# A head loop with the last head's DMA transposes turned back to TensorE, its loads on one queue, and a few steps moved by half a product

## The chip, the core and the metric

The kernel runs on one core of a Trainium2 chip. The metric is the device time of one execution in microseconds (us); lower is better. The core has TensorE (PE, its weight loads shown as PEld), VectorE (DVE), ScalarE (ACT), GpSimd (POOL) and SyncE (SP), each with an instruction queue of its own that it works off in order. DMAs are issued by SyncE and, some, by GpSimd.

## What is computed

Two layers of a decoder trunk over 1024 tokens of width 1024: dilated attention and an MLP, then gated linear attention and an MLP. The change lies in the first layer's attention. Cut to that:

```python
DILATED_GROUPS = ((128, 1), (512, 4), (2048, 16))   # three branches g = 0, 1, 2; 8 heads of 128
def dilated_attention(h, w_in, w_out):
    qkv = (h @ w_in).reshape(B, S, N_GROUPS, 3, ATTN_HEADS, HEAD_DIM)
    for g, (window, dil) in enumerate(DILATED_GROUPS):
        q = apply_rope(qkv[:, :, g, 0], cos, sin) * (HEAD_DIM ** -0.5)
        k = apply_rope(qkv[:, :, g, 1], cos, sin)
        o_g, lse_g = dilated_group_attention(q, k, v, dil, window // dil)
    alpha = jax.nn.softmax(jnp.stack(lses, axis=0), axis=0)
    o = jnp.sum(alpha[..., None] * jnp.stack(outs, axis=0), axis=0)
    return o.reshape(B, S, ATTN_WIDTH).astype(h.dtype) @ w_out
```

## The kernel before, in words

Values are made earlier. The head loop (`Heads.run_head`, L1184) then runs through 24 groups p = 3h + g, one for each head h and branch g. A group makes q and k of its head and branch as one 2 x 2 block product by a Strassen-Winograd scheme with seven products, S0 to S6 in the order of SLOTS: S0 into bank X, S1 into Y, S3 into V, S2 onto X, S6 onto V, S4 onto X, S5 into Z. (The names in the trace: pX<-s2 is S2, pX<-s3 is S4, pV<-s4 is S6.) Each fp32 product is three matmuls of rounded parts (high and low). Every product is issued in two halves, and after each half `advance` (L947) moves a clock by one and issues what an agenda holds for that step, in order of rank, the lower first. A group has 14 steps; c is its first, so c + 14 is step 0 of the next group. The agenda fixes only the order in each engine's queue: an engine that is not waiting runs ahead of the clock.

In a group with start c (`Heads.plan`, L1158): `keep` copies bank X by ScalarE to e1, e2, e3 (steps 3, 9, 13) and V to e5 (step 7); TensorE may add to X again only when the copy before it has been made. `column` (L1124) adds two banks into a quarter of q or k and issues two DMAs (`cw<-c`, L1130 and L1131) that swap its upper and lower 64 partitions; four steps later VectorE's `turn` (L1138, L1139, L1146) applies the rotary tables and writes qT or kT. One column, of q, is due in step c + 15, that is step 1 of the next group. `load` (L1115) fetches the weights of the next group by four DMAs of 256 KB in step 1, `stage` cuts them from step 8 on.

Attention of a group follows one group later (`follow`, L1196; `Attention.plan`, L1084), in four pairs of query blocks j = 0 to 3: scores (L989) from step 8, softmax on VectorE and ScalarE (L1003, L1005), then P must be transposed. For the second branch TensorE does it (`turn`, L1016, with ScalarE's copy L1018). For the first and third branch it is done by DMA: ScalarE splits P into 16-bit halves (L1035), GpSimd's queue writes them to DRAM (`pscr`, L1037), and SyncE issues a DMA transpose back (`flip`, L1048). Then TensorE multiplies P by V (`values`, L1069), ScalarE copies the result (`orow`, L1073) and SyncE stores it to `og`. Entries of POINTS are the steps of scores, turn or halves, values, and flips.

From the second group of the next head on, `plan_merges` (L1302) merges a head's three branches: it loads the rows of `og` (L1209, 780 KB, half 0 in step 0 of the third group), VectorE computes the weights (L1216, L1217, L1222 to L1225), ScalarE scales twelve slices (L1229, steps 6 to 9), VectorE adds them, and SyncE stores to `oscr`.

In the last group, p = 23, the output projection's weights (`W.dma`, 4 x 512 KB) and the first merged rows (`ol`, 1 MB, L1294) are loaded through GpSimd's queue in steps 1 to 3; ScalarE and VectorE prepare the weights in steps 5 to 8 (L152, L153), and TensorE transposes `ol` in step 8 (L260). `tail` (L1781) spreads the attention of group 23 over the output projection's blocks; two steps of the agenda run after each block.

Of the kernel before, what the change touches and what calls it, by code (L numbers as in the profile page):

```python
# [20 lines left out]
P = 128  # L21
# [4 lines left out]
HEADS = 8  # L26
HD = 128
AW = HEADS * HD
NG = 3
# [13 lines left out]
def hybrid_trunk(ctx, tc, x, norm_mix, norm_mlp, norm_fin, a_in, a_out, g_in, g_up, g_b, g_nw,  # L43
                 g_out, m_up, m_down, tab, msk, gmask, ident_d, out):
    nc = tc.nc
    pe, act, dve, pool, sp = nc.tensor, nc.scalar, nc.vector, nc.gpsimd, nc.sync
# [7 lines left out]
    def h8(shape, dt, name):  # L54
        return wk.tile(shape, dt, name=name, tag="h8", bufs=12)

    def k4(shape, dt, name):
        return wk.tile(shape, dt, name=name, tag="k4", bufs=25)

    def t2(shape, dt, name):  # L60
        return wk.tile(shape, dt, name=name, tag="t2", bufs=8)
# [50 lines left out]
    class Weights:  # L112
# [14 lines left out]
            self.slots.append(src)  # L127
            self.by.append(by)

        def dma(self, by=None):  # L130
            n = self.ndma
            if n < len(self.slots):
                self.ndma += 1
                src = self.slots[n]
                self.raws[n] = k4([P] + list(src.shape[1:]), F32, "raw")
                (by or sp).dma_start(self.raws[n], src)

        def prep(self, eng=dve):
            n = self.nprep
# [41 lines left out]
    W = Weights()  # L181
# [8 lines left out]
    def add_rows(w, k0, by=None):  # L190
        for k in range(2):
            W.add(w[P * (k0 + k):P * (k0 + k + 1), :], by and by(k0 + k))
# [93 lines left out]
    class Split:  # L286
# [4 lines left out]
        @staticmethod  # L291
        def at(tiles, k):
            n = 4 // len(tiles)
            return tiles[k // n][:, k % n, :]
# [442 lines left out]
    oscr = drp.tile([S, D], F32, name="oscr")  # L737
# [209 lines left out]
    def advance():  # L947
        clock[0] += 1
        for _, fn in sorted(agenda.pop(clock[0], []), key=lambda e: e[0]):
            fn()  # L950
# [9 lines left out]
    def load_values(g, h):  # L960

        v = k4([P, NB, HD], F32, "v")
        c = slice(HD * h, HD * h + HD)
        if g == 0:
            sp.dma_start(v, vscr.rearrange("(b p) g c -> p b g c", p=P)[:, :, 0, c])
        elif g == 1:
            for b in range(2):
                sp.dma_start(v.rearrange("p (r b) c -> p r b c", b=2)[:, :, b, :],
                             vscr[512 * b:512 * b + 512].rearrange("(p r) g c -> p r g c", r=4)[:, :, 1, c])
        else:  # L970
            sp.dma_start(v, vscr.rearrange("(p r) g c -> p r g c", r=8)[:, :, 2, c])
        return v
# [6 lines left out]
    class Attention:  # L979
# [102 lines left out]
                    sp.dma_start(to.rearrange("(p r) c -> p r c", r=8)[:, 2 * j - 2:2 * j + 2, :], row)  # L1082

        def plan(self, c, points, turn, values, flip=None):  # L1084
            self.by_dma = flip is not None and self.g in (0, 2)
            if flip is not None and not self.by_dma:
                turn, values = (12, 12, 16, 16), (16, 16, 18, 18)

            def get():
                self.v = load_values(self.g, self.h)  # L1090
            at(c + points[0] - 2, get)
            for j in range(4):
                t = c + points[j]
                at(t, lambda j=j: self.scores(j), 2)
                at(t + 1 + (j % 2 and points[j] == points[j - 1]), lambda j=j: self.soft(j), 2)
                if self.by_dma:
                    at(c + turn[j], lambda j=j: self.halves(j), 3)
                    at(c + flip[j], lambda j=j: self.flip(j), 3)
                else:
                    at(c + turn[j], lambda j=j: self.turn(j), 3)  # L1100
                at(c + values[j], lambda j=j: self.values(j), 4)

    class Heads(Up):
# [54 lines left out]
        def plan(self, p):  # L1158
            c = 14 * p
            st = self.st.setdefault(p, {})  # L1160
            self.behind = True

            def keep(b, name):
                def fn():
                    e = t2([P, 512], F32, name)
                    act.activation(e, st[b], AF.Copy)  # L1166
                    st[name] = e
                return fn
            at(c + 3, keep("X", "e1"), 0)
            at(c + 5, lambda: self.column(p, 0, 0, st["Y"], st["e1"]), 1)  # L1170
            at(c + 7, keep("V", "e5"), 0)
            at(c + 9, keep("X", "e2"), 0)
            at(c + 11, lambda: self.column(p, 1, 0, st["V"], st["e2"]), 1)
            at(c + 13, keep("X", "e3"), 0)
            at(c + 13, lambda: self.column(p, 1, 1, st["X"], st["e5"]), 1)
            at(c + 15, lambda: self.column(p, 0, 1, st["Z"], st["e3"]), 1)
            if p == 0:
                for s, t in ((4, 1), (6, 3), (5, 5)):
                    at(c + t, lambda s=s: self.stage(p, s), 7)
            at(c + 1, lambda: self.load(p + 1))  # L1180
            for s, t in ((0, 8), (1, 9), (2, 10), (3, 11), (4, 14), (6, 15), (5, 17)):
                at(c + t, lambda s=s: self.stage(p + 1, s), 7)

        def run_head(self, p):  # L1184
            self.plan(p)
            if p:
                self.follow(p - 1, 14 * p, self.POINTS if p < self.count - 1 else self.SINGLE)
            for s in self.SLOTS:
# [1 line left out]
                    self.product(p, s, range(2 * half, 2 * half + 2))  # L1190
                    advance()

        POINTS = (8, 8, 12, 12), (11, 12, 15, 16), (21, 21, 25, 25), (14, 15, 18, 19)
        SINGLE = (8, 10, 12, 14), (12, 14, 16, 18), (14, 16, 18, 20)

        def follow(self, p, c, points):  # L1196
# [91 lines left out]
                reached.add((0, half))  # L1288
            at(clock[0] + 7, last)

    def ahead_h8(pairs, by=sp):

        t = h8([P, 4, 512], F32, "ol")
        by.dma_start(t, oscr[512 * pairs:512 * pairs + 512, 0:512].rearrange("(b p) c -> p b c", p=P))  # L1294
        return [t[:, 0:2, :], t[:, 2:4, :]]

    def ahead_k4(p):
# [4 lines left out]
    def plan_merges(h, c):  # L1302

        rows, part = {}, {}

        def load(half):
            rows[half] = merge_load(h, half)

        def weigh(half):
            part[half] = merge_weights(rows[half])  # L1310

        def join(half):
            del part[half]
            merged(h, half, merge_join(rows.pop(half), dve))
        for half in range(2):
            t = c + 14 + 11 * half
            at(t, lambda half=half: load(half))
            if half and h == HEADS - 2:
                t += 8
            at(t + 4, lambda half=half: weigh(half), 9)  # L1320
            at(t + 5, lambda half=half: merge_shares(rows[half], *part[half]), 9)
            for n in range(4):
                at(t + 6 + n, lambda half=half, n=n: merge_scale(rows[half], part[half][1], n), 9)
            at(t + 10, lambda half=half: join(half), 9)
# [383 lines left out]
    for i, n in enumerate(plan[:-5]):  # L1708
# [5 lines left out]
        if n == vals.STEPS - 2:  # L1714
            heads = Heads(vals.h)
# [38 lines left out]
    ol = []  # L1754
    turned = Turned(ol, x[0])
    for p in range(heads.count):
        h, g = divmod(p, NG)
        if g == 1 and h:
            plan_merges(h - 1, 14 * p)
        if p == heads.count - 1:  # L1760
            for k in range(0, KT, 2):
                add_rows(a_out, k)
            c = 14 * p
            at(c + 1, lambda: (W.dma(pool), W.dma(pool)), 0)
            at(c + 2, lambda: (W.dma(pool), W.dma(pool)), 0)
            at(c + 3, lambda: ol.extend(ahead_h8(0, pool)), 0)
            for t in (5, 6, 7, 8):
                at(c + t, lambda: W.prep(dve), 7)
            at(c + 8, lambda: turned.turn(0), 7)
            at(c + 9, lambda: (turned.load_x(0), turned.load_x(1)))  # L1770
            at(c + 11, lambda: turned.turn(1), 7)
            at(c + 17, lambda: ol.extend(ahead_h8(1)), 9)
        heads.run_head(p)
# [7 lines left out]
    def tail():  # L1781

        c = clock[0]
        heads.follow(heads.count - 1, c, ((6, 7, 8, 9), (9, 10, 11, 12), (11, 12, 13, 14)))
        load, start, finish = merges(HEADS - 1, merged)
        rows = {}
        advance()

        def early(half):
            t = rows[half] = h8([P, 4, 512], F32, "ol2")  # L1790
            sp.dma_start(t[:, :, 0:384], oscr[512 * half:512 * half + 512, 512:896].rearrange("(b p) c -> p b c", p=P))
        at(c + 7, lambda: early(0))
        at(c + 16, lambda: early(1))
        for i, (half, h) in enumerate(((0, 4), (0, 5), (0, 6), (1, 4), (1, 5), (1, 6))):
            at(c + (13 + 3 * i if half == 0 else 21 + i), lambda half=half, h=h: t_head(h, half, rows[half][:, :, HD * (h - 4):HD * (h - 4) + HD]))
        at(c + 15, lambda: (load(0), load(1)), 9)
        at(c + 18, lambda: start(0))
        at(c + 19, lambda: finish(0))
        at(c + 20, lambda: start(1))
        at(c + 21, lambda: finish(1))  # L1800
        steps.extend([advance] * 42)

    tail()


# [587 lines left out]
    ol, turn1 = [], []  # L2393
# [81 lines left out]
```

## Time and profile before

| | us |
|---|---|
| median of 3 runs (lowest, highest) | 2601.3 (2597.0, 2602.2) |
| the profiled execution, by its own time | 2598.5 |
| its span | 2596.7 |
| TensorE busy | 2574.3 (99%) |
| VectorE busy | 1864.0 (72%) |
| ScalarE busy | 1298.7 (50%) |
| mean granted TensorE clock | 0.998 |

How to read the lines that follow. A line of the timeline has the start and the length in us, the engine, the source line, the operation and out<-in by the program's names; in brackets stands the idle time of the engine just before it and what ended it. An engine's name with a q is its sequencer, so SPq is the issue of a DMA by SyncE. A line of the waits has who waited for whom, us in total, times, and the longest. A line of the windows has the stretch, its length, and the busy time (and number) of PE, PEld, DVE, ACT and POOL, then the granted clock of TensorE, the busy share of the DMA engines and GB/s. A line of the DMA view has queue, number, KB each, and the median us from issue to landing.

### The profile page before, as it was taken

The page shows a single profiled execution, that of the slowest core. Times are in us where ns is not written, and L with a number is a line of the kernel's source. Part 1 is how long each engine was busy: PE and PEld are TensorE (multiplying, and loading weights), DVE is VectorE, ACT ScalarE, POOL GpSimd, SP SyncE. Part 2 cuts the span into 40 slices and gives each one's busy share as a digit, 9 for nine tenths or more (in the row PEclk, how much of TensorE's full clock was granted, in tenths as well). Part 3 has the DMA queues.
Part 4 walks back from the last instruction along what each step waited for, and adds up shares of the span by engine and source line. Part 5 has one row for each costly group of instructions (what it writes and reads, how often), then busy time and mean ns, then how long its engine had stood idle before and what let it go on. Part 6 is the DMA issues. An engine that isn't in the chain of part 4 may idle for free.

```text
span 2596.7 us, 33212 instructions
## 1 busy us (share of the span) xinstructions
PE 2574.3 (99%) x11985; PEld 2142.2 (82%) x11985; DVE 1864.0 (72%) x3018; ACT 1298.7 (50%) x2360; POOL 51.8 (2%) x81
## 2 busy tenths in 40 slices
PE   9999999999998999999999999999999999999998
PEld 7888888888887888888888888888888888888887
DVE  7745888888887768666657587887657866656567
ACT  6423455656655446555534345654326554553334
POOL 0000000000001000000000000000000000000000
PEclk9999999999999999999999999999999999999999
DMA  5543677777778633554775452463513544396543
GB/s 183 170 141 115 153 179 200 176 201 196 196 205 221 208 122 127 170 168 139 278 260 182 140 195 96 133 200 98 195 65 118 170 157 155 130 356 203 183 149 131
DMA packets 377911, 445.70 MB, mean 172 GB/s; under 512 B 68145, under 2 KB 240561, under 8 KB 377746
## 3 DMA queue, kind: packets, MB, share of 16 engines
q1 hardware_dynamic: 372850, 428.63, 53.5%
q0 software_dynamic: 4752, 14.68, 1.7%
q8 instruction: 94, 1.54, 0.2%
q14 instruction: 71, 0.58, 0.1%
q10 hardware_dynamic: 144, 0.26, 0.0%
HBM read 279.19 MB, written 127.60 MB: 157 GB/s over the span
## 4 chain that ended last, share of the span: by engine, by line
PE 65%; DVE 3%; ACT 1%; DMA 1%; issue 1%; SPq 0%; DVEq 0%; ACTq 0%
PE pB L1938 13%; PE pX L599 10%; PE pA L1938 10%; PE pV L599 7%; PE pY L599 3%; PE pZ L599 3%; PE pd L216 3%; PE pd L214 3%; PE pd L215 3%; PE pB L830 3%; PE pA L830 2%; PE pT L335 1%; DMA cw<-c 1%; PE pO L2236 1%; PE pU L2218 0%
## 5 line engine op out<-in xcount | busy, mean ns | idle before, releaser
L1938 PE MATMUL pB<-dh 128*128 128x512 f32 x512 | 199.4, 389 | 0.0
L1938 PE MATMUL pB<-dh,dl 128*128 128x512 f32 x512 | 199.2, 389 | 0.0
L1938 PE MATMUL pB<-dl,dh 128*128 128x512 f32 x512 | 199.2, 389 | 0.0
L223 DVE TENSOR_TENSOR dl<-sin,dh 128x1024 fp32r<-128x1024 f32 x112 | 136.8, 1221 | 42.4 <-ACT dh L220 41.8
L220 ACT ACTIVATE dh<-sin 128x1024 fp32r<-128x1024 f32 x112 | 117.8, 1052 | 88.4 <-PE pB L1938 33.4
L220 ACT ACTIVATE dh<-kept 128x1024 fp32r<-128x1024 f32 x64 | 67.9, 1061 | 183.3 <-DVE kept L1903 138.1
L599 PE MATMUL pV<-s4h,wd 128*128 128x512 f32 x448 | 150.3, 397 | 0.0
L1938 PE MATMUL pA<-dl,dh 128*128 128x512 f32 x384 | 149.4, 389 | 0.0
L1938 PE MATMUL pA<-dh,dl 128*128 128x512 f32 x384 | 149.4, 389 | 0.0
L1938 PE MATMUL pA<-dh 128*128 128x512 f32 x384 | 149.4, 389 | 0.0
L1005 ACT ACTIVATE pt<-pt,orow 128x128 f32<-128x128 f32 (+1 forms) x192 | 84.7, 443 | 75.7 <-DVE orow L1003 74.4
L1938 PEld LDWEIGHTS pB<-dh 128*128 128x128 f32 x512 | 96.2, 188 | 19.9
L1938 PEld LDWEIGHTS pB<-dl,dh 128*128 128x128 f32 x512 | 96.2, 188 | 19.9
L1938 PEld LDWEIGHTS pB<-dh,dl 128*128 128x128 f32 x512 | 96.1, 188 | 19.8
L537 DVE TENSOR_TENSOR wal<-raw,wah 128x512 fp32r<-128x512 f32 x112 | 76.2, 687 | 40.8 <-ACT wah L536 40.8
L537 DVE TENSOR_TENSOR wbl<-t,wbh 128x1024 fp32r<-128x1024 f32 x56 | 68.6, 1225 | 43.9 <-ACT wbh L536 43.8
L599 PEld LDWEIGHTS pV<-s4h,wd 128*128 128x128 f32 x448 | 84.2, 188 | 19.3 <-ACT e L1166 1.7
L608 ACT ACTIVATE c<-c 128x512 f32<-128x512 f32 x64 | 40.4, 631 | 118.6 <-DVE c L636 77.5
L223 DVE TENSOR_TENSOR dl<-kept,dh 128x1024 fp32r<-128x1024 f32 x64 | 78.4, 1225 | 24.7 <-ACT dh L220 18.7
L599 PE MATMUL pX<-s3h,wgh 128*128 128x512 f32 x224 | 89.3, 399 | 2.4 <-ACT e L1166 2.4
L599 PE MATMUL pZ<-a22h,wgh 128*128 128x512 f32 x224 | 90.1, 402 | 0.0
L599 PE MATMUL pX<-s2h,wbh 128*128 128x512 f32 x224 | 89.0, 397 | 0.0
(400 smaller groups left out, 7378.7 us busy)
## 6 DMA issues: line engine op xcount, KB each, us to landing
sin<-acts SPq DMA_DIRECT2D x112, 512.0 KB, 3.9
raw<-in_mlp_w_up_dram SPq DMA_DIRECT2D x64, 512.0 KB, 6.0
acts<-s SPq DMA_DIRECT2D x64, 512.0 KB, 3.5
raw<-in_mlp_w_down_dram SPq DMA_DIRECT2D x64, 512.0 KB, 4.8
raw<-in_attn_w_in_dram SPq DMA_DIRECT2D x98, 256.0 KB, 4.7
cw<-c SPq DMA_DIRECT2D x192, 128.0 KB, 2.8
acts<-c SPq DMA_DIRECT2D x64, 256.0 KB, 2.2
kept<-in_mlp_w_down_dram SPq DMA_DIRECT2D x32, 512.0 KB, 5.8
```

Of the source, the lines that this page charges most:

```text
L214: pe.matmul(ps, sh, mh, start=start, stop=False)
L215: pe.matmul(ps, sh, ml, start=False, stop=False)
L216: pe.matmul(ps, sl, mh, start=False, stop=stop)
L220: act.activation(hi, src, AF.Copy)
L223: dve.tensor_tensor(lo, src, hi.bitcast(F32), op=OP.subtract)
L335: pe.transpose(ps[:, k, 128 * i:128 * i + 128], xn[i][:, c:c + 128], ident)
L537: self.remain(lambda: dve.tensor_tensor(lo, src, hi.bitcast(F32), op=OP.subtract))
L599: pe.matmul(st[b], u[:, k, :], v, start=first and k + n == 0, stop=k == 3 and n == 2, skip_group_check=True)
L608: act.activation(r, r, AF.Relu)
L830: pe.matmul(self.acc[s][t], a[:, c], b[:, k, :], start=fresh and m + k + v == 0, stop=m == 1 and k == 1 and v == 2, skip_group_check=True)
L1005: act.activation(pt[:, i, :128 * n], pt[:, i, :128 * n], AF.Exp, scale=-1.0, bias=m, accum_out=self.row[:, r, HD:HD + 1])
L1938: pe.matmul(self.acc[s][t], a[:, k, c], b[:, k, :], start=fresh and m + k + v == 0, stop=m == 7 and k == 1 and v == 2, skip_group_check=True)
```

## The change

- The first branch of head 7 is no longer transposed by DMA but by TensorE (`by_dma` also asks for h < 7); its steps become those of the second branch.
- The flips of the other branches: j = 1 moves from step 15 to 14, j = 3 from 19 to 18, so that each pair of flips stands in one step.
- The load of the next group's weights moves from step 1 to step 3.
- The copy e2 of bank X moves from step 9 to step 8 in groups with p mod 3 = 1, but for p = 22.
- The loads of the output weights and of `ol` in group 23 are issued by SyncE instead of GpSimd, in the same steps.
- In the tail, scores, turns and values of group 23 come one step later.

```diff
         def plan(self, c, points, turn, values, flip=None):
-            self.by_dma = flip is not None and self.g in (0, 2)
+            self.by_dma = flip is not None and self.g in (0, 2) and self.h < HEADS - 1
             if flip is not None and not self.by_dma:
                 turn, values = (12, 12, 16, 16), (16, 16, 18, 18)
...
-            at(c + 9, keep("X", "e2"), 0)
+            at(c + (8 if p % NG == 1 and p < self.count - 2 else 9), keep("X", "e2"), 0)
...
-            at(c + 1, lambda: self.load(p + 1))
+            at(c + 3, lambda: self.load(p + 1))
...
-        POINTS = (8, 8, 12, 12), (11, 12, 15, 16), (21, 21, 25, 25), (14, 15, 18, 19)
+        POINTS = (8, 8, 12, 12), (11, 12, 15, 16), (21, 21, 25, 25), (14, 14, 18, 18)
...
-            at(c + 1, lambda: (W.dma(pool), W.dma(pool)), 0)
-            at(c + 2, lambda: (W.dma(pool), W.dma(pool)), 0)
-            at(c + 3, lambda: ol.extend(ahead_h8(0, pool)), 0)
+            at(c + 1, lambda: (W.dma(), W.dma()), 0)
+            at(c + 2, lambda: (W.dma(), W.dma()), 0)
+            at(c + 3, lambda: ol.extend(ahead_h8(0)), 0)
...
-        heads.follow(heads.count - 1, c, ((6, 7, 8, 9), (9, 10, 11, 12), (11, 12, 13, 14)))
+        heads.follow(heads.count - 1, c, ((7, 8, 9, 10), (10, 11, 12, 13), (12, 13, 14, 15)))
```

`W.dma` and `ahead_h8` lose the argument that named the queue; both then issue on SyncE.

More of the change, by code (lines that the diff above doesn't have):

```diff
@@ L128, in add, with dma @@
             self.by.append(by)
-        def dma(self, by=None):
+        def dma(self):
             n = self.ndma
@@ L135, in dma @@
                 self.raws[n] = k4([P] + list(src.shape[1:]), F32, "raw")
-                (by or sp).dma_start(self.raws[n], src)
+                sp.dma_start(self.raws[n], src)
         def prep(self, eng=dve):
@@ L1289, in merged, with ahead_h8 @@
             at(clock[0] + 7, last)
-    def ahead_h8(pairs, by=sp):
+    def ahead_h8(pairs):
         t = h8([P, 4, 512], F32, "ol")
-        by.dma_start(t, oscr[512 * pairs:512 * pairs + 512, 0:512].rearrange("(b p) c -> p b c", p=P))
+        sp.dma_start(t, oscr[512 * pairs:512 * pairs + 512, 0:512].rearrange("(b p) c -> p b c", p=P))
         return [t[:, 0:2, :], t[:, 2:4, :]]
```

## The prediction

> **What bounds the kernel now.** I read the page's busy times first, then TensorE's waits, then windows and timelines around each wait.
>
> ```profile
> span 2596.7 us, 33212 instructions
> PE 2574.3 (99%) x11985; PEld 2142.2 (82%) x11985; DVE 1864.0 (72%) x3018; ACT 1298.7 (50%) x2360; POOL 51.8 (2%) x81
> ```
>
> TensorE is busy 99% of the span, so an edit gains only where it ends one of TensorE's waits, and loses where it starts one or gives TensorE more work. The waits of the head loop are three lines:
>
> ```profile
> PE pO L1069 <- DMA pt<-pscr: 7.0, 5, 5.4
> PE pX L599 <- ACT e L1166: 2.4, 7, 1.1
> PE pS L989 <- DVE qT L1146: 2.2, 3, 1.7
> ```
>
> One wait of 5.4 us is far longer than the rest: TensorE, about to multiply P by V, waits for a DMA transpose (a flip). The timeline puts it into the last group, p = 23, where the flips of head 7's first branch come due. (Groups are called first, second and third by p mod 3.)
>
> ```profile
> 814.84 1.15 POOL L136 DMA_DIRECT2D raw<-in_attn_w_out_dram  x2
> 819.71 1.22 POOL L136 DMA_DIRECT2D raw<-in_attn_w_out_dram  x2
> 821.12 10.34 SPq L1048 DMA_TRANSPOSE pt<-pscr  x2
> 832.63 2.07 PE L1069 MATMUL pO<-v,pt 128*128 128x128 f32 x8 [5.41 <-DMA pt<-pscr]
> 843.25 0.50 PE L599 MATMUL pX<-s3h,wgh 128*128 128x512 f32 x1 [1.08 <-ACT e L1166]
> ...
> 832.00:834.00 2.00, 1.37 (x6) 1.37 (x7) 1.97 (x3) 1.25 (x2) 0.00 (x0) 0.50 1.18 377
> 834.00:836.00 2.00, 2.00 (x8) 1.71 (x7) 1.90 (x6) 0.00 (x0) 0.00 (x0) 0.50 1.02 352
> 836.00:838.00 2.00, 2.00 (x10) 1.61 (x10) 1.35 (x2) 1.84 (x5) 0.00 (x0) 0.73 1.21 163
> ```
>
> Two flips hold SyncE's queue for 10.34 us while 2 MB of output weights land: the DMA share behind the clock column is above 1. TensorE stands 5.41 us, and then runs at a granted clock of 0.50 and 0.73.
>
> The five waits on flips are 7.0 us in all, so the other four hold 1.6 us; they lie in third groups of heads 1 to 6. What sets those groups is another thing. Here are two of them, p = 11 and, below the dots, p = 8:
>
> ```profile
> 514.16 2.51 SPq L1048 DMA_TRANSPOSE pt<-pscr  x2
> 516.77 0.53 SPq L1209 DMA_DIRECT2D rows<-og  x1
> 517.93 0.58 SPq L1131 DMA_DIRECT2D cw<-c  x1
> 518.60 1.95 SPq L1048 DMA_TRANSPOSE pt<-pscr  x1
> 524.02 0.69 DVE L1138 TENSOR_TENSOR cw<-cw,tab 128x512 f32<-128x512 f32 x1 [0.45 <-DMA cw<-c]
> 526.98 0.17 DVE L1225 TENSOR_TENSOR me<-me,mz 128x12 f32<-128x12 f32 x1
> 527.18 0.99 ACT L1229 ACTIVATE rows<-rows,me 128x128 f32<-128x128 f32 x3 [3.97 <-DVE me L1225]
> 530.84 0.69 DVE L1138 TENSOR_TENSOR cw<-cw,tab 128x512 f32<-128x512 f32 x1 [1.86 <-DMA cw<-c]
> 531.31 0.58 ACT L1166 ACTIVATE e<-pX 128x512 f32<-128x512 f32 x1
> 531.94 0.50 PE L599 MATMUL pX<-s3h,wgh 128*128 128x512 f32 x1 [0.20 <-ACT e L1166]
> ...
> 448.01 0.69 DVE L1138 TENSOR_TENSOR cw<-cw,tab 128x512 f32<-128x512 f32 x1 [1.13 <-DMA cw<-c]
> 449.03 1.16 PE L1069 MATMUL pO<-v,pt 128*128 128x128 f32 x8 [0.55 <-DMA pt<-pscr]
> 455.77 0.69 DVE L1138 TENSOR_TENSOR cw<-cw,tab 128x512 f32<-128x512 f32 x1 [2.86 <-DMA cw<-c]
> 455.94 0.50 PE L599 MATMUL pX<-s3h,wgh 128*128 128x512 f32 x1 [0.22 <-ACT e L1166]
> ```
>
> VectorE waits for the swapped rotary rows `cw`, finishes qT, then the merge weights `me`; ScalarE scales the merge rows, and behind them in its queue stands e2, the copy of bank X that TensorE needs. From VectorE's start on cw to TensorE's start on pX it is 531.94 - 524.02 = 7.92 us in the one group and 455.94 - 448.01 = 7.93 in the other, though only the second had a flip wait (0.55). So the landing of cw sets the group; the flip wait lies inside that chain and is worth nothing by itself.
>
> **The change part by part.**
>
> *Head 7 without flips.* Gone are the stand of 5.41 us and the slow clock after it: 1.37 x 0.5 + 2.00 x 0.5 + 2.00 x 0.27 = 2.2 us. Head 7's first branch now needs 3 + 4 + 4 + 4 = 15 transposes on TensorE, 7 in p = 22 and 8 in p = 23. Their price is that of the second branch's transposes:
>
> ```profile
> 770.36 0.82 PE L1016 MATMUL pP<-ident,pt 128*128 128x128 f32 x6
> 771.02 1.50 PE L1069 MATMUL pO<-v,pt 128*128 128x128 f32 x12
> ```
>
> (771.02 - 770.36) / 6 = 0.11 us each, 1.7 us in all, without a new break, since they stand beside scores or values that are there anyway. ScalarE loses the five `halves` and gets four copies. The e2 wait of 1.08 us should fall towards the 0.2 of other third groups: the `orow` copy leaves ScalarE's queue there, but four weight preparations stay. I take 0.9. Sum: -5.4 - 2.2 + 1.7 - 0.9 = **-6.8 us**, with ends at -8.5 (the transposes wholly in slack) and -4 (third rival below).
>
> The rule on the clock in the Trainium skill, TensorE: Matmul & The Clock Gate, Part 1, is that about 3.4 us of idling halve the rate; this trace agrees with its 5.41 us and 0.50, and by the rule none of the waits under 2 us that this change shifts would cost clock.
>
> *Output weights and `ol` from GpSimd's queue to SyncE's.* Four loads and one of 1 MB now stand in SyncE's order, ahead of cw (steps 1 and 5), og and v of p = 23. The trace has the same loads from both queues:
>
> ```profile
> raw<-in_attn_w_out_dram POOLq DMA_DIRECT2D x4, 512.0 KB, 8.9
> raw<-in_attn_w_out_dram SPq DMA_DIRECT2D x4, 512.0 KB, 10.3
> ...
> ol<-oscr POOLq DMA_DIRECT2D x1, 1024.0 KB, 7.9
> ol<-oscr SPq DMA_DIRECT2D x1, 1024.0 KB, 8.2
> ```
>
> 8.9 against 10.3 and 7.9 against 8.2 us to land: about equal. With the five flips of p = 23 gone the queue has room, so I take 0; the upper end is priced as a rival.
>
> *Flips (14, 15, 18, 19) to (14, 14, 18, 18).* In the second and third groups the flip of j = 1 moves ahead of cw of step 1, in third groups ahead of the 780 KB of `rows` too, and the flip of j = 3 ahead of cw of step 5. Queued behind them is everything VectorE's chain waits for. Two flips took 2.51 us of SyncE's queue, so one holds cw back by up to 1.26; the other end is 0, if its transfer hides in DMA time that is idle before rows start (first rival). I take 1.0, nearer the flip's own row. In the six third groups with merges (heads 1 to 6) the chain passes it on whole: **+6.0 us**, ends 0 and +8. The four flip waits go, but what is late next is cw, so they bring nothing. A gain is excluded there unless the chain is wrong (a rival). In second groups TensorE has no wait and no merge stands in ScalarE's queue. Of p = 13, a window row gives its length and the busy time of PE, PEld, DVE, ACT and POOL:
>
> ```profile
> 565.70:589.90 24.20, 24.20 (x118) 20.45 (x117) 20.07 (x42) 14.01 (x34) 3.28 (x5) 1.00 0.76 187
> ```
>
> Busy 24.20 of 24.20 us: 0 from the flips there.
>
> A rule of the Trainium skill speaks against this edit: DMA: Bandwidth & Descriptors, Queues, rings and completion order, says that each engine takes the descriptors of one queue row in ring order. By it the whole transfer of the flip precedes rows and cw and the term would be its upper end; no run here yet shows it.
>
> *Loads of the next weights from step 1 to step 3.* Four DMAs pass the cw of step 1 and, in second and third groups, nothing else that is not moved too; in first groups they pass one og store of two DMAs. They are read at step 8. 0 to +1 us in all, I take 0.
>
> *e2 half a product sooner in second groups.* The row above shows no wait of TensorE in such a group to take away, and the groups that wait (p = 8, 11) are third groups, which the edit leaves alone. ScalarE's weight cut of step 8 comes later by one copy, 0.6 us, and its reader is a group away: 0.
>
> *Tail one step later.* Scores j = 0 waited for qT:
>
> ```profile
> 863.61 0.68 PE L989 MATMUL pS<-kT,qT 128*128 128x128 f32 x4 [1.74 <-DVE qT L1146]
> 864.13 0.83 PE L1069 MATMUL pO<-v,pt 128*128 128x128 f32 x6
> 864.80 0.61 PE L989 MATMUL pS<-kT,qT 128*128 128x128 f32 x4
> ```
>
> Steps 6 and 7 run in the same tick, after the same block, so the scores stay there; only the pO that stood behind them comes first and fills 864.80 - 864.13 = **0.7 us** of the wait (ends 0 and -1.7).
>
> Sum: -6.8 + 6.0 - 0.7 = **-1.5 us**. The profiled execution took 2598.5 us (its span and 1.8 around it), so 2597.0; it lies 2.8 below the median of the runs, 2601.3, on which scale I forecast **2599.8**. Below, 0.2% (5.2 us) is about what a measurement can tell from no change.
>
> **The rivals.**
>
> *Faster: the flips cost nothing.* If the flip of j = 1 runs in DMA time that is idle before rows start, and cw lands as before, only -6.8 - 0.7 = -7.5 is left, and the flip waits may add up to 1.6: 2592 to 2594. For it: SyncE issues rows at 516.77 with only the flips before it. Against: VectorE waits for cw in both groups shown, so no slack absorbs a later issue. Chance 0.22.
>
> *Slower: the second pair of flips carries into the next group.* The cw of step 5 was late too (waits of 1.86 and 2.86 us in the two groups). If the flip of j = 3 ahead of it delays VectorE's scores and merge sums beyond what TensorE itself has lost, the next first group starts late by up to 2.86 - 1.86 = 1.0 us. Six times 1.3 and six times 1.0, less 7.5: +6.3 us, 2607.6. It decides from 2.1 us a head on. Against: TensorE is late by about the same. Chance 0.10.
>
> *The change does not free p = 23.* `ol` behind 2 MB of weights and rows on one queue: it took 8.2 us to land, and TensorE transposes it at step 8, some 14 us into the group. If SyncE gets to it 3 us later than there is room for, TensorE waits for ol in place of the flip, the first term shrinks to -4, and the sum is +1.3: 2602.6. Chance 0.15; it stays within 0.2%.
>
> **How the numbers follow.** The forecast has 0.53. Within 0.2% lie the forecast and the third rival: 0.68; faster 0.22, slower 0.10. The likeliest case's own range, with the flips between +2.3 (where the sum leaves 0.2%) and +8, is -5.2 to +0.5, 2596.1 to 2601.8. The range to hold 8 in 10 takes in the third rival and most of the first: 2593.5 to 2604.5.
>
> **What would show it.** Right: no pO wait on flips in p = 23, clock 1.00 there, 15 more pP transposes; in third groups rows and cw issued about 1.3 us later against the flips, VectorE's wait for cw near 2 us, and the group longer by as much though its pO waits are gone; second groups still 24.2 us. Wrong: third groups as long as before (faster rival), first groups longer by 1 us (slower rival), a pT wait on ol (third rival), or a new wait in second groups.

## The result and the profile after

The changed kernel takes **2629.6 us** (four runs, 2627.8 to 2632.0) against 2600.7 of the kernel before beside it (2597.0 to 2602.2): ratio 1.0114, 95% interval 1.0096 to 1.0131. It is 29 us slower; the forecast was 1.5 us faster, and its range ended at 2604.5. The page of the changed kernel begins so:

```profile
span 2626.3 us, 33210 instructions
...
PE 2583.6 (98%) x12000; PEld 2150.3 (82%) x12000; DVE 1863.9 (71%) x3018; ACT 1296.5 (49%) x2359; POOL 45.5 (2%) x71
```

The work is the same but for 15 matmuls more; the span has grown by 29.6 us. TensorE's waits (who for whom, us in total, times, longest):

```profile
PE pS L989 <- DVE qT L1146: 29.7, 8, 5.9
PE pT L260 <- DMA ol<-oscr: 1.6, 1, 1.6
PE pV L599 <- ACT e L1166: 0.9, 1, 0.9
```

The waits on flips are gone, and the e2 waits in third groups nearly so. In their place the scores wait for qT, 29.7 us where it was 2.2. To see where, I added the lengths of the groups, each from its first matmul to the next group's:

| us | first groups (p = 3 to 21) | second (4 to 22) | third (5 to 20) | p = 23 and all after |
|---|---|---|---|---|
| before | 172.1 | 169.1 | 161.7 | 1779.9 |
| changed | 170.3 | 169.9 | **198.0** | 1774.8 |
| difference | -1.8 | +0.8 | **+36.3** | -5.1 |

Together +30.2; what lies ahead of the groups makes it 29.6. The last group gained 5.1 us; the forecast had 7.5 for it. The six third groups, forecast at +6, lost 36. Here is p = 11 of the changed kernel, which starts at 523.8 (before, the same group started at 514.9): SyncE's queue, then VectorE, then TensorE.

```profile
526.57 3.86 SPq L1048 DMA_TRANSPOSE pt<-pscr  x3
530.52 0.53 SPq L1209 DMA_DIRECT2D rows<-og  x1
531.16 0.61 SPq L1130 DMA_DIRECT2D cw<-c  x1
531.82 0.58 SPq L1131 DMA_DIRECT2D cw<-c  x1
...
538.48 0.17 DVE L1216 TENSOR_REDUCE mz<-rows 128x4 f32<-128x12 f32 x1 [3.33 <-DMA rows<-og]
539.59 0.69 DVE L1138 TENSOR_TENSOR cw<-cw,tab 128x512 f32<-128x512 f32 x1
542.53 0.17 DVE L1225 TENSOR_TENSOR me<-me,mz 128x12 f32<-128x12 f32 x1
...
542.05 2.50 PE L989 MATMUL pS<-kT,qT 128*128 128x256 f32 x6 [5.41 <-DVE qT L1146]
```

Set against the group's start, the flips begin at 2.8 us (before: -0.7), rows are issued at 6.7 (before: 1.9), and VectorE, which now waits for rows and not for cw, ends me at 18.9 (before: 12.3). So the group inherits 3.5 us of lateness, loses 1.3 more to the third flip ahead of rows, and 2.6 more until rows land. The DMA view gives that last part: rows of p = 11, us from issue to landing, before and below it changed.

```profile
rows<-og SPq DMA_DIRECT2D x1, 780.0 KB, 5.3
```
```profile
rows<-og SPq DMA_DIRECT2D x1, 780.0 KB, 7.9
```

3.5 + 1.3 + 2.6 = 7.4 us; the group is 33.3 - 26.5 = 6.8 us longer. TensorE's clock falls too (windows of the changed kernel; the value behind POOL is the granted clock):

```profile
538.00:540.00 2.00, 0.00 (x0) 0.00 (x0) 1.36 (x4) 0.21 (x1) 0.00 (x0) 0.73 1.19 267
540.00:542.00 2.00, 0.00 (x0) 0.00 (x0) 1.97 (x4) 0.00 (x0) 0.00 (x0) 0.50 1.40 267
542.00:544.00 2.00, 1.95 (x6) 1.60 (x6) 1.24 (x8) 1.27 (x4) 0.00 (x0) 0.50 1.11 233
```

Little of that slow stretch shows in the time of this group: me came 6.6 us later and the group is 6.8 longer, so 0.2 is left for the clock. Over the six third groups it is 2.8 of the 36.3 us (worked out below).

Two edits could bring such lateness: the load in step 3 and the flips in pairs. The theory that I formed first was the load (the lateness is there before the group starts); its rivals were the flips, and both together.

### The profile page after: what moved, and what is told of

The parts are those of the page before. It is cut to its first block, busy times and chain, and to the rows that moved or that the text cites. A ratio compares the mean times of both kernels' runs of the same rounds, so it can differ in the third digit from the quotient of the medians.

```text
span 2626.3 us, 33210 instructions
## 1 busy us (share of the span) xinstructions
PE 2583.6 (98%) x12000; PEld 2150.3 (82%) x12000; DVE 1863.9 (71%) x3018; ACT 1296.5 (49%) x2359; POOL 45.5 (2%) x71
## 4 chain that ended last, share of the span: by engine, by line
PE 84%; DVE 6%; DMA 5%; ACT 2%; issue 1%; SPq 1%; DVEq 0%; ACTq 0%
PE pX L599 14%; PE pB L1938 13%; PE pA L1938 10%; PE pV L599 9%; PE pB L830 7%; PE pA L830 5%; PE pZ L599 5%; PE pY L599 5%; PE pd L216 3%; PE pd L214 3%; PE pd L215 3%; DMA rows<-og 2%; DMA cw<-c 1%; PE pS L989 1%; PE pO L1069 1%
## 5 line engine op out<-in xcount | busy, mean ns | idle before, releaser
L989 PE MATMUL pS<-kT,qT 128*128 128x128 f32 (+1 forms) x384 | 76.9, 342 | 29.7 <-DVE qT L1146 29.7
L1138 DVE TENSOR_TENSOR cw<-cw,tab 128x512 f32<-128x512 f32 x96 | 65.8, 686 | 53.6 <-DMA cw<-c 53.4
L223 DVE TENSOR_TENSOR dl<-kept,dh 128x1024 fp32r<-128x1024 f32 x64 | 78.4, 1225 | 24.4 <-ACT dh L220 18.4
L989 PEld LDWEIGHTS pS<-kT,qT 128*128 128x128 f32 x384 | 62.8, 201 | 38.8 <-DVE qT L1146 30.5
```

Source lines behind the costliest of these rows:

```text
L223: dve.tensor_tensor(lo, src, hi.bitcast(F32), op=OP.subtract)
L989: pe.matmul(ps[:, i, :128 * n], self.qT[:, 128 * b:128 * b + 128], self.kT[:, k0:k0 + 128 * n], start=True, stop=True)
L1138: dve.tensor_tensor(w, w, ctab[:, 1, sl], op=OP.mult)
```

## The experiments

**Each of the two undone, and each alone.** The changed kernel with the load back:

```diff
-            at(c + 3, lambda: self.load(p + 1))
+            at(c + 1, lambda: self.load(p + 1))
```

> The changed kernel with the load of the next weights back in step 1. The third groups of heads 1 to 6 (p = 5, 8, 11, 14, 17, 20) lost about 36 us in the changed kernel while its other edits should have brought 7.5. Load theory: the four load DMAs, now right ahead of cw of step 5, delay its landing by some 4 us in first groups; SyncE and VectorE stay late through the second group and the third group pays. By it the loss goes down to the flips' 6 us: 2598 to 2602 us, SyncE's flips of second groups start within 0.5 us of where they did before, and third groups last about 28 us. Flips theory: the pairs of flips alone cost the 36 us: it stays at 2626 to 2632 and third groups last 33 us. Joint theory: each moves the same queue late and it runs over only with both: 2598 to 2612, and then undoing the flips alone brings as much.

The changed kernel with the flips back:

```diff
-        POINTS = (8, 8, 12, 12), (11, 12, 15, 16), (21, 21, 25, 25), (14, 14, 18, 18)
+        POINTS = (8, 8, 12, 12), (11, 12, 15, 16), (21, 21, 25, 25), (14, 15, 18, 19)
```

> The changed kernel with the flips back in steps 14, 15, 18, 19, the load left in step 3. Load theory: third groups still last 32 to 33 us, 2618 to 2626 us. Flips theory: 2591 to 2595, third groups near 27 us. Joint theory: 2593 to 2606.

The kernel before with only the load in step 3 (the first diff the other way round):

> The kernel before with the load in step 3 and nothing else changed. Load theory: 2625 to 2634 us (about 30 above the kernel before), cw of step 5 landing about 4 us later in the first groups of heads 2 to 6, waits of TensorE for qT in third groups of 4 us and more. Flips theory: 2599 to 2603. Joint theory: 2600 to 2612.

The kernel before with only the flips in pairs (the second diff the other way round):

> The kernel before with the flips in steps 14, 14, 18, 18 and nothing else changed. Load theory: the forecast's own +6 us, 2604 to 2610, third groups near 28 us. Flips theory: 2634 to 2640, third groups near 33 us. Joint theory: 2603 to 2614.

| kernel | median us | ratio to before, interval | third groups, us | p = 23 and after |
|---|---|---|---|---|
| changed, load back | 2617.4 | 1.0066 (1.0051 to 1.0081) | 191.2 | 1773.8 |
| changed, flips back | 2610.9 | 1.0044 (1.0029 to 1.0058) | 179.8 | 1775.3 |
| before + load | 2618.3 | 1.0066 (1.0051 to 1.0081) | 179.9 | 1781.4 |
| before + flips | 2623.6 | 1.0088 (1.0073 to 1.0103) | 182.8 | 1785.1 |

No theory of a single cause holds, and none of the four times lies in a range that was expected. Alone, the load costs 18.4 us and the flips 23.7, of which some 5 lie in the last group, where the changed kernel has no flips. My first theory, the load, held for half of the loss.

**Both undone.** The changed kernel with both diffs applied:

> The changed kernel with the load back in step 1 and the flips back in 14, 15, 18, 19: what is left is head 7 without flips, the queue of the output weights, e2 and the tail. If the loss lies in the load and the flips alone, the forecast's other terms hold: 2600 less 7.5, 2590 to 2595 us, third groups near 27 us. If e2 or the queue of the output weights holds part of the loss, 2598 and more, with a new wait of TensorE in second groups or in the last group.

2593.2 us, ratio 0.9972 (0.9960 to 0.9984): 7.1 us faster than before. Third groups last 162.7 us in all, as before. So the whole loss is in the load and the flips: against this kernel the load costs 2610.88 - 2593.24 = 17.6, the flips 2617.37 - 2593.24 = 24.1, and both 36.4, five less than their sum.

**Where the load costs.** The load in step 3 in first groups alone:

```diff
-            at(c + 1, lambda: self.load(p + 1))
+            at(c + (3 if p % NG == 0 else 1), lambda: self.load(p + 1))
```

> The kernel before with the load in step 3 in first groups only (p mod 3 = 0), in step 1 elsewhere. Theory of the og store: in first groups alone the load falls behind an og store that waits for ScalarE's orow of step 2, so its four DMAs start 4.5 us later and cw of step 5 lands 3 to 4 us later; this holds the whole price of the load, 2614 to 2620 us. Rival, DMA traffic: the load costs wherever it stands nearer to cw of step 5 or to the flips, so that a third of the groups holds about a third: 2604 to 2608.

2618.8 us, ratio 1.0069 (1.0052 to 1.0086): the whole price lies in the first groups. SyncE's queue in the first group p = 9, before, and below it with this edit (groups start at 465.3 and 467.3):

```profile
470.70 2.24 SPq L1121 DMA_DIRECT2D raw<-in_attn_w_in_dram  x4
474.17 4.36 SPq L1079 DMA_DIRECT2D og<-orow  x4
478.63 0.47 SPq L1130 DMA_DIRECT2D cw<-c  x1
```
```profile
476.84 0.88 SPq L1079 DMA_DIRECT2D og<-orow  x2
477.81 2.13 SPq L1121 DMA_DIRECT2D raw<-in_attn_w_in_dram  x4
480.05 1.40 SPq L1079 DMA_DIRECT2D og<-orow  x2
481.54 1.74 SPq L1130 DMA_DIRECT2D cw<-c  x1
483.32 0.60 SPq L1131 DMA_DIRECT2D cw<-c  x1
```

The og store of step 2 waits for ScalarE's orow, 9 us into the group. Before, the load passed ahead of it at 5.4 us into the group and its megabyte moved while SyncE waited. Now it starts at 10.5, and cw of step 5 lands behind it, at 20.6 us into the group where it was 16.1. VectorE's `turn`, before, and below it with this edit, in p = 9 and in the second group p = 10:

```profile
482.27 0.69 DVE L1138 TENSOR_TENSOR cw<-cw,tab 128x512 f32<-128x512 f32 x1
...
503.90 0.69 DVE L1138 TENSOR_TENSOR cw<-cw,tab 128x512 f32<-128x512 f32 x1
```
```profile
487.95 0.69 DVE L1138 TENSOR_TENSOR cw<-cw,tab 128x512 f32<-128x512 f32 x1 [2.93 <-DMA cw<-c]
...
510.30 0.69 DVE L1138 TENSOR_TENSOR cw<-cw,tab 128x512 f32<-128x512 f32 x1 [3.46 <-DMA cw<-c]
```

VectorE is 3.7 us late (487.95 - 467.3 = 20.7 against 17.0), so it makes the next column late, SyncE issues that column's cw late and everything behind it, and the cw of the second group is late again: 17.0 us into p = 10 against 13.2. TensorE does not feel it: second groups still last 24.16 us in nearly all heads. The third group does:

```profile
520.49 2.52 SPq L1048 DMA_TRANSPOSE pt<-pscr  x2
523.10 0.53 SPq L1209 DMA_DIRECT2D rows<-og  x1
524.89 2.20 SPq L1048 DMA_TRANSPOSE pt<-pscr  x1
...
531.77 1.86 PE L1069 MATMUL pO<-v,pt 128*128 128x128 f32 x8 [3.35 <-DMA pt<-pscr]
```

Rows are issued 5.0 us into p = 11 (before: 1.9), and TensorE waits over 3 us for the flip of j = 1. A delay of one engine pair went through 24 us of a group that showed full load of TensorE, and was paid one group later.

**Is it the og store, or the nearness to cw of step 5?** The load in step 2, ahead of the store:

```diff
-            at(c + 1, lambda: self.load(p + 1))
+            at(c + 2, lambda: self.load(p + 1), 0)
```

> The kernel before with the load in step 2 and at the head of that step, so that no og store stands ahead of it, though cw of step 5 still comes right behind the loads and one store. Theory that the load pays only where it waits behind the og store: 2599 to 2604 us, cw of step 5 in first groups lands within 0.5 us of before. Theory that any nearness to cw of step 5 costs: a third to a half of the price in step 3, 2606 to 2610.

2601.1 us, ratio 1.0004 (0.9994 to 1.0014): free. Its queue in p = 9 (start 465.5):

```profile
471.58 2.23 SPq L1121 DMA_DIRECT2D raw<-in_attn_w_in_dram  x4
474.54 3.67 SPq L1079 DMA_DIRECT2D og<-orow  x4
478.60 0.47 SPq L1130 DMA_DIRECT2D cw<-c  x1
```

cw of step 5 landed 1.1 us later than before, not within the 0.5 expected, and cost nothing. So one step is free, and the next one, past a store that waits, is worth 18 us.

**Which flip costs.** Only j = 1 moved, then only j = 3:

```diff
-  ... (14, 15, 18, 19)
+  ... (14, 14, 18, 19)
```

> The kernel before with the flips in 14, 14, 18, 19: only j = 1 moves. The flips alone cost 23.7 us, of which the trace puts 21 into the third groups and 5 into the last. Theory that j = 1 ahead of rows and cw of step 1 is the whole price: 2618 to 2625 us, third groups near 30 us. Theory that both pairs carry half: 2608 to 2614.

```diff
-  ... (14, 15, 18, 19)
+  ... (14, 15, 18, 18)
```

> The kernel before with the flips in 14, 15, 18, 18: only j = 3 moves, ahead of cw of step 5. Theory that j = 1 is the whole price: 2598 to 2603 us. Theory that cw of step 5 lands late, and with it the next group: 2606 to 2612, the second groups or first groups longer by 1 us.

j = 1 alone: 2625.8 us, ratio 1.0097 (1.0072 to 1.0123), third groups 187.8 us. That is as much as both flips cost, or more. j = 3 alone: 2608.8 us, ratio 1.0034 (1.0021 to 1.0047), third groups 161.7 as before, but first groups 179.7 where they were 172.1. I expected the one or the other to be zero; both have a price of their own, in different groups, and they don't add: once the third group is late, the first one behind it has room. With j = 3 alone, in p = 8 and p = 9 (VectorE, then ScalarE and TensorE):

```profile
456.24 0.69 DVE L1138 TENSOR_TENSOR cw<-cw,tab 128x512 f32<-128x512 f32 x1 [3.72 <-DMA cw<-c]
...
472.78 0.21 ACT L1218 ACTIVATE me<-md 128x12 f32<-128x12 f32 x1 [4.45 <-DVE md L1217]
473.42 1.60 PE L1069 MATMUL pO<-v,pt 128*128 128x128 f32 x12 [1.03 <-ACT pt L1018]
```

VectorE's wait for cw of step 5 is 3.72 us (2.86 before), and in the next group VectorE is still late: it begins the merge weights of the second half 7.8 us into p = 9, 6.9 before. ScalarE waits for them (md), the copy of the transposed P stands behind that in its queue, and TensorE waits 1.03 us for the copy (0.35 before). The steps between cw and the merge weights were not followed one by one. This is the second rival of the forecast, seen by itself: it put up to 1.0 us on each head, and (179.7 - 172.1) / 6 is 1.3.

**The flips the other way.** All four behind cw:

```diff
-  ... (14, 15, 18, 19)
+  ... (15, 15, 19, 19)
```

> The kernel before with the flips in steps 15, 15, 19, 19, the pair behind cw instead of ahead of it. Theory that a flip costs cw its whole transfer (some 3 us a group for the one flip moved the other way): cw lands 2 to 3 us sooner, TensorE then waits about 1 us for the flips: 2587 to 2595 us. Theory that a flip costs cw its time in SyncE's queue alone: 2595 to 2602, cw 1.3 us sooner at most.

2593.2 us, ratio 0.9969 (0.9956 to 0.9982): 7.1 us faster than the kernel before, in the range of the first theory. cw of step 1 landed 3.2 us sooner on average (6.4 us into the third groups, 9.6 before). p = 8 starts at 436.8 here:

```profile
436.58 0.36 SPq L1209 DMA_DIRECT2D rows<-og  x1
438.31 0.46 SPq L1130 DMA_DIRECT2D cw<-c  x1
438.82 0.59 SPq L1131 DMA_DIRECT2D cw<-c  x1
439.52 4.19 SPq L1048 DMA_TRANSPOSE pt<-pscr  x3
...
444.55 0.17 DVE L1216 TENSOR_REDUCE mz<-rows 128x4 f32<-128x12 f32 x1
445.45 0.68 DVE L1138 TENSOR_TENSOR cw<-cw,tab 128x512 f32<-128x512 f32 x1
```

Rows are issued as the group starts, VectorE waits for neither rows nor cw, and third groups last 26.0 to 26.5 us (156.9 in all, 4.8 less than before; first groups gain 1.9). TensorE has no wait in them above 0.23 us. No wait for a flip is left there that matters: all but 0.2 us of the 8.9 that remain lie in the last group.

**cw or rows?** Rows one step later, behind cw of step 1:

```diff
-            at(t, lambda half=half: load(half))
+            at(t + (not half), lambda half=half: load(half), 5 if half else 2)
```

> The kernel before with the 780 KB of merge rows, half 0, one step later, behind cw of step 1 and ahead of the flip of j = 1. Theory that the landing of cw behind rows sets the third groups: cw lands 3 us sooner, the chain to ScalarE starts by the landing of rows, 1 us later than before, and me ends some 2 us sooner: six times 2, 2585 to 2591 us. Rival, that rows themselves set me: no more than the 1 us, which is against it: 2600 to 2607.

2611.6 us, ratio 1.0044 (1.0029 to 1.0059): slower, against my expectation. cw landed 4 us sooner and VectorE did not profit, because the first step of the merge weights (L1216), which stands ahead of `turn` in its queue, waits for rows (here in p = 8; in the other five groups 2.9 to 3.5 us):

```profile
447.92 0.17 DVE L1216 TENSOR_REDUCE mz<-rows 128x4 f32<-128x12 f32 x1 [0.94 <-DMA rows<-og]
```

So the forecast's chain begins at whichever of rows and cw lands last, and "the landing of cw sets the group" was half of it. From me on, the chain holds throughout: in 64 of the 66 third groups of all eighteen kernels in which TensorE's clock stayed at 1.00, the group ended 14.2 us after me (14.16 to 14.21), whether me ended 11.8 or 15.3 us into the group. This run also shows a second part of the price. Counted from the DMA packets of the trace, rows take 3.7 to 4.3 us from first packet to last in the third groups before, with 131 to 217 KB of GpSimd's queue (the halves going to `pscr`) moved in between. With the flips in pairs they take 5.1 to 5.9, with 262 to 270 KB in between. Here, with no flip of j = 1 ahead, five groups take 5.1 to 5.7 with 262 KB, and one, p = 8, takes 3.6 with 168 KB; that one lasted 26.95 us, the other five 28.9 to 29.5. With the flips behind cw, the four groups with none in between take 2.8 to 3.2. And where rows and `pscr` are late together (load in first groups alone) it is 4.0 to 4.5. So rows that start 1.4 us later, while GpSimd's queue does not, run into its write. That the write stretches them is read from these counts; no run removed the write itself.

**The edits of the last group, and e2.** Head 7 without flips, alone:

> The kernel before with nothing but head 7 without flips; output weights and ol stay on GpSimd's queue. The forecast's term is -6.8 us (ends -8.5 and -4): 2593 to 2594 us, no wait for a flip in the last group, its clock 1.00. If the new queue for the weights was part of that gain, less than -6; if it hurt (a wait of 1.1 us on ol in the last group of the kernels with it), more than -7.5.

The same with output weights and `ol` on SyncE's queue:

> The kernel before with head 7 without flips and with output weights and ol on SyncE's queue; e2 and tail as before. Head 7 alone was worth 4.0 us, with queue, e2 and tail together 7.1. If the queue gives the difference, by an earlier landing of the merge rows in the last group: 2592.5 to 2594. If the tail's step does: 2596 to 2597.

e2 alone:

> The kernel before with nothing but the copy e2 in step 8 of second groups. Forecast: 0, 2599 to 2602 us, second groups 24.16 us as before. Rival, the copy ahead of the weight cut delays ScalarE into the third group: +1 to +3 us.

e2 with the flips in pairs:

> The kernel before with the flips in 14, 14, 18, 18 and e2 in step 8 of second groups. In the profile with the load back, which has both, third groups were 1.4 us longer on average than with the flips alone. If e2 does it by delaying ScalarE: 2628 to 2633 us. If that was a difference between two executions: 2621 to 2626.

Their edits are those lines of the diff shown above. Head 7 alone: 2596.4 us, ratio 0.9984 (0.9975 to 0.9993), 4.0 us gained. With the queue: 2592.8, ratio 0.9973 (0.9962 to 0.9984), 6.9 us. Rows of p = 23 (DMA view), with the weights on GpSimd's queue and below on SyncE's:

```profile
rows<-og SPq DMA_DIRECT2D x1, 780.0 KB, 8.0
```
```profile
rows<-og SPq DMA_DIRECT2D x1, 780.0 KB, 5.0
```

On the one queue rows stand ahead of the weights and land in 5.0 us; on two, both move at once and rows take 8.0. TensorE then waits for ScalarE's e5 and e2, which it does not with one queue:

```profile
836.82 0.50 PE L599 MATMUL pV<-s4h,wd 128*128 128x512 f32 x1 [0.92 <-ACT e L1166]
841.91 0.50 PE L599 MATMUL pX<-s3h,wgh 128*128 128x512 f32 x1 [1.42 <-ACT e L1166]
```

e2 alone: 2601.0 us, ratio 1.0003 (0.9993 to 1.0012); with the flips: 2625.0, ratio 1.0100 (1.0085 to 1.0116), beside 1.0088 without it. Nothing in either case. Since the kernel with both undone (e2 and the tail's step beside head 7 and the queue) is at 2593.2, the tail's step is worth nothing that can be measured either.

**The two gains together.** The changed kernel with the load back in step 1 and the flips in 15, 15, 19, 19:

> The changed kernel with the load back in step 1 and the flips in 15, 15, 19, 19. The two gains lie in different groups (head 7 and tail in the last, flips behind cw in the third groups of heads 1 to 6), so they should add: 2600 less 7 and less 7, 2584 to 2588 us. If the flips behind cw gained part of their 7 us in the last group, where head 7 has no flips here, 2588 to 2592.

2585.6 us (2583.8 to 2586.3), ratio 0.9943 (0.9928 to 0.9957): 14.8 us faster than the kernel before, where the two gains add to 14.2. Its page:

```profile
span 2584.2 us, 33191 instructions
...
PE 2570.5 (99%) x12000; PEld 2142.1 (83%) x12000; DVE 1862.5 (72%) x3018; ACT 1296.6 (50%) x2359; POOL 45.5 (2%) x71
```

## Why the prediction was wrong

Two steps failed. *The load* is the one: "Four DMAs pass the cw of step 1 and, in second and third groups, nothing else that is not moved too; in first groups they pass one og store of two DMAs. ... 0 to +1 us in all, I take 0." It measured 18 us. With the load alone the third groups are 18.2 us longer: 12.9 because me is later, 5.3 behind me, in groups with TensorE's clock at 0.50. The store was named but counted as two issues. What mattered of it was how long it waits, and it waits for orow. The load in step 2 shows the size of the mistake: up to that store the move is free.

*The flips* are the other: "Two flips took 2.51 us of SyncE's queue, so one holds cw back by up to 1.26 ... I take 1.0 ... +6.0 us, ends 0 and +8." It measured 24 us. The chain from me on was right: a late landing goes through VectorE, me and ScalarE into the group whole. The upper end was wrong, since it took the flip's time in the queue for all that it costs. Measured in third groups, as three separate parts: 1.4 us of issue, 0.9 until the first packet of rows (1.2 us after its issue before, 2.0 to 2.1 with the flip ahead), and about 1.5 because rows then run beside GpSimd's write: 3.8 us; the group is 3.5 us longer on average (182.8 - 161.7, over 6). cw, which stands behind rows, landed 3.0 us later (12.6 us into the group, 9.6 before) and me ended 3.1 later; the other 0.4 lies behind me, in groups with TensorE's clock at 0.50. With the ring order that the Trainium skill gives (DMA: Bandwidth & Descriptors, Queues, rings and completion order) the 0.9 agrees: the flip's transfer goes first. I had cited that rule as speaking for the upper end and then sized the transfer by the issue. The same page of the Trainium skill says under Issuing engines are not separate DMA queues that transfers of GpSimd and SyncE share the same engines and interleave; the 5.0 and 8.0 us of p = 23 agree.

*Second groups*: "0 from the flips there" held for the length of second groups (169.1 us in all with the flips alone, as before), and is what misled: "Busy 24.20 of 24.20 us" shows that TensorE lost nothing there, not that VectorE and SyncE did not.

*The rival of the carried second pair* (chance 0.10) was real by itself, 7.6 us more in first groups for 6 priced, but in the changed kernel it is covered by the third group's own loss: first groups there were 1.8 us shorter.

*The clock*: "by the rule none of the waits under 2 us that this change shifts would cost clock." Wrong, as shown below. The slow clock goes with little of the changed kernel's loss (2.8 of 36.3 us in third groups), but with 5.3 us of the load's and 8.7 of the flips' in the changed kernel with the load back.

*Head 7*: -6.8 forecast, -4.0 measured, its end. The e2 wait of 1.08 us did not fall by 0.9: with the output weights still on GpSimd's queue, waits of 0.92 and 1.42 us for ScalarE's copies stand there. *The queue*: 0 forecast, -2.9 measured (6.9 less 4.0). I compared how long the weights take from either queue, and not what they do to rows on the other. Together -6.9: two mistakes that cancel, and it is luck that this sum lies near the forecast. The third rival's wait for `ol` did come (1.1 to 1.6 us), and was outweighed. *e2*: 0, right. *Tail*: -0.7 forecast, none seen.

Sum by the measured terms: -6.9 for the last group, +36.4 for load and flips together: +29.5, against 28.9 measured.

With both flips moved, third groups lasted 182.8 and 182.7 us in two kernels, 191.2 in the changed one with the load back, which differs from them in nothing that lies in those groups but e2, and the second of the two has that. The traces split this. A third group with the clock at 1.00 ends 14.2 us after me; one with 3.4 us at 0.50 ended 14.2 to 15.6 after it (28 groups), one with 6.8 us 14.2 to 16.8 (14 groups). What goes beyond 14.2 adds up to 2.5 and 3.3 us in the two kernels and 8.7 in the third (2.8 in the changed kernel, 5.3 with the load alone), where three of six groups have the longer stretch (one and none in the two); the remaining 2 us are a later me. Open: each kernel has one profiled execution, and whether a stretch lasts 3.4 or 6.8 us hangs on fractions of a microsecond (last section), so how much of the 8.7 belongs to the kernel is not shown.

## What to carry to other kernels

Before moving a DMA issue, look at each instruction that it comes to stand behind and at how long that one waits: here a store of two DMAs that waited for ScalarE turned a free move into 18 us. A group in which the busiest engine never waits can still hand on a delay, so follow the other engines' start times through it to the first group that has a wait. Price a transfer put ahead of another by the landing of the one behind it, and ask which other queue's traffic it will now meet.

## What the hardware showed that I had not expected

TensorE's clock fell after stands far shorter than the one of 5.41 us. With flips and e2, p = 8 had a stand of 1.56 us and then one of 0.85 (TensorE's timeline, then windows of 3.41 us; the granted clock stands behind POOL's busy time):

```profile
455.24 1.35 PE L989 MATMUL pS<-kT,qT 128*128 128x256 f32 x6 [1.56 <-DVE qT L1146]
457.44 0.80 PE L599 MATMUL pV<-s4h,wd 128*128 128x512 f32 x1 [0.85 <-ACT e L1166]
```
```profile
453.86:457.27 3.41, 1.35 (x6) 0.90 (x6) 2.54 (x10) 1.34 (x4) 0.00 (x0) 1.00 1.39 216
457.27:460.69 3.42, 3.25 (x8) 2.57 (x9) 0.14 (x1) 3.42 (x11) 0.00 (x0) 0.50 1.07 251
```

Some 3.6 us after the stand began, with TensorE at work again, it ran at 0.50 for 3.4 us. All 18 stands of 1.56 to 2.97 us in third groups of the three kernels with j = 1 moved and the load in step 1 (flips alone, flips and e2, j = 1 alone) were followed by 0.50, for 3.4 us or for 6.8; behind the waits of 0.2 to 0.6 us in third groups of the kernel before it stays at 1.00. The length of a stand does not decide alone: one of 1.83 us (load alone, p = 8) was not followed by 0.50, and neither were four of 1.68 to 1.75 (rows one step later). Here is the longest of the four, 1.75 us up to 605.43, in p = 14:

```profile
601.94:605.35 3.41, 1.74 (x11) 1.39 (x9) 0.97 (x4) 0.21 (x1) 0.00 (x0) 1.00 1.20 193
605.35:608.77 3.42, 3.34 (x21) 3.02 (x22) 2.95 (x8) 0.39 (x2) 0.00 (x0) 1.00 1.21 288
```

The traces show what goes with it. In each run with more than one, the slow stretches of the head loop begin whole multiples of 3.413 us apart (with flips and e2 at 378.77 and 457.27, 23 of them) and last one to four of these. The windows above are cut on that grid: 1.35 us of work in the first pair, 1.74 in the second. Counted so from 340 to 880 us of all eighteen kernels, the 52 windows at full clock in which TensorE was idle for more than 1.8 us were all followed by one at 0.50, the 2702 with less than 1.65 never, and three of the seven between. Of the windows at 0.50, the 32 with more than 0.55 us idle were all followed by another, the 55 with less never. So it is TensorE's idle time within such a window, as the profile has it, that goes with the clock of the next, and a stand that falls across two windows counts in parts. The rule on the clock that the prediction cited (the Trainium skill, TensorE: Matmul & The Clock Gate, Part 1) has about 3.4 us of idling; about half of that, within one window, was enough here.
